# A DMA-bound multiply and GELU: a wider small piece, its x load split in two, and three waits changed

## The chip, the core and the metric

The kernel runs on one core of a Trainium2 chip. The metric is the device time of one execution in microseconds (us). Three runs of the kernel before gave 119.72, 119.79 and 119.87 us; the median is 119.79 us.

## The reference

Two float32 arrays of 1024 x 4096 are multiplied element by element, and the tanh form of GELU is applied to the product.

```
z = x * y
return 0.5 * z * (1 + np.tanh(np.sqrt(2 / np.pi) * (z + 0.044715 * z ** 3)))
```

Each array has 16.78 MB. x and y are read once and the result is written once, so 50.33 MB cross between the chip's DRAM and the core's on-chip memory.

## The kernel before

The kernel treats each array as a flat stretch of 4,194,304 numbers and cuts it into three **pieces**, given in columns of a 128-row tile: piece 0 is columns 0 to 1280, piece 1 is 1280 to 17664, piece 2 is 17664 to 32768 (`PIECES`). A piece is one unbroken stretch of DRAM, and each of the 128 rows (partitions) holds one unbroken part of it. A row of piece 0 is 5 KB long, a row of piece 1 is 64 KB, a row of piece 2 is 59 KB. The trace's records of the DMA traffic have one packet for each row, of that size.

All of x stays on chip, in the tile `xs` of 32768 columns. The products and the GELU are written back into `xs`, and the stores read it. y has a smaller buffer, `ys`, of 20440 columns, so its parts must share room. In the text below x0, x1, x2 are the x loads of pieces 0, 1, 2. y0, y1, y2 are the y loads in their order in `Y_LOADS`, which is another order: y0 belongs to piece 1, y1 to piece 2 and y2 to the small piece 0. The stores o0, o1, o2 follow that same order (`STORES`): piece 1, piece 2, piece 0.

The third number in `Y_LOADS` is the column of `ys` where a part starts. y0 lies at 4056 to 20440. y1 lies at 0 to 15104 and so overlaps y0, and y2 lies at 15104 to 16384. `Y_FREE` says how many products must be done before a y load may be issued: none for y0, three for y1, four for y2.

Two queues issue DMAs. Each DMA is spread over the same 16 DMA engines, and each engine works through the packets of one queue in order.

- ScalarE's queue issues x1 only. `_hoist` moves this issue ahead of the barrier with which the program opens.
- SyncE's queue (SP) issues everything else. x0 is hoisted in the same manner. After the barrier SP waits until x0 has landed, issues y0 and x2, waits for three products, issues y1, waits for the fourth, issues y2, waits for y1's landing (line 114) and for the GELUs of piece 1, issues o0, then o1 and o2 as their GELUs finish. At the end it waits for the stores.

VectorE forms the products (line 98) in the steps of `STEPS`: four steps of 4096 columns for piece 1, seven of 2048 and one of 768 for piece 2, one of 1280 for piece 0. Before a piece's first step it waits for its x and y. ScalarE follows each product with the GELU (line 106). `sem_mul` counts products and `sem_act` counts GELUs; each DMA adds 16 to its semaphore when all of it has landed.

Of the kernel before, what the change touches and what calls it, by code (L numbers as in the profile page):

```python
# [1 line left out]

# [4 lines left out]


F32 = mybir.dt.float32
GELU = mybir.ActivationFunctionType.Gelu_apprx_tanh  # L10

PIECES = [(0, 1280), (1280, 17664), (17664, 32768)]

Y_LOADS = [(1280, 17664, 4056), (17664, 32768, 0), (0, 1280, 15104)]

Y_FREE = [0, 3, 4]

STEPS = [[4096] * 4, [2048] * 7 + [768], [1280]]  # L20
STORES = [(1280, 17664), (17664, 32768), (0, 1280)]
Y_BUF = 20440


def _hoist(nc, issued):

    here = nc.cur_bb.bb.instructions
    first = nc.main_func.blocks[0].instructions
    for ins in issued:
        del here[next(k for k, i in enumerate(here) if i is ins or i.name == ins.name)]  # L30
    engine = issued[0].engine
    at = next(
        k
        for k, i in enumerate(first)
        if i.engine == engine and type(i).__name__ == "InstDrain"
    )
    first[at:at] = issued


@with_exitstack  # L40
def kernel(
    ctx: ExitStack,
    tc: tile.TileContext,
    x: bass.AP,
    y: bass.AP,
    out: bass.AP,
):
    nc = tc.nc
    P = nc.NUM_PARTITIONS

    def columns(t, a, b):

        flat = t.flatten_outer_dims().rearrange("r c -> (r c)")
        pa, pb = next(q for q in PIECES if q[0] <= a and b <= q[1])
        return flat[P * pa : P * pb].rearrange("(p c) -> p c", p=P)[:, a - pa : b - pa]


    tc.close()
    tc.compile()  # L59

    xs = nc.alloc_sbuf_tensor("xs", [P, PIECES[-1][1]], F32).ap()
    ys = nc.alloc_sbuf_tensor("ys", [P, Y_BUF], F32).ap()
    sem_x = [nc.alloc_semaphore(f"sem_x{i}") for i in range(len(PIECES))]
    sem_y = [nc.alloc_semaphore(f"sem_y{i}") for i in range(len(Y_LOADS))]
    sem_mul = nc.alloc_semaphore("sem_mul")
    sem_act = nc.alloc_semaphore("sem_act")
    sem_o = [nc.alloc_semaphore(f"sem_o{i}") for i in range(len(STORES))]

    def load_x(i, engine=nc.sync):
        a, b = PIECES[i]  # L70
        return engine.dma_start(out=xs[:, a:b], in_=columns(x, a, b)).then_inc(sem_x[i], 16)

    def load_y(i):
        a, b, r = Y_LOADS[i]
        return nc.sync.dma_start(
            out=ys[:, r : r + b - a], in_=columns(y, a, b)
        ).then_inc(sem_y[i], 16)

    _hoist(nc, [load_x(0).ins])
    _hoist(nc, [load_x(1, nc.scalar).ins])  # L80
    nc.sync.wait_ge(sem_x[0], 16)
    load_y(0)
    load_x(2)
    for i in range(1, len(Y_LOADS)):
        if Y_FREE[i]:
            nc.sync.wait_ge(sem_mul, Y_FREE[i])
        load_y(i)

    n = 0
    done = {}  # L90
    for i, (a, b, r) in enumerate(Y_LOADS):
        for j, (xa, xb) in enumerate(PIECES):
            if xa <= a < xb:
                nc.vector.wait_ge(sem_x[j], 16)
        nc.vector.wait_ge(sem_y[i], 16)  # L95
        c = a
        for w in STEPS[i]:
            nc.vector.tensor_mul(  # L98
                out=xs[:, c : c + w],
                in0=xs[:, c : c + w],  # L100
                in1=ys[:, r + c - a : r + c - a + w],
            ).then_inc(sem_mul, 1)
            n += 1
            done[c + w] = n
            nc.scalar.wait_ge(sem_mul, n)
            nc.scalar.activation(  # L106
                out=xs[:, c : c + w], in_=xs[:, c : c + w], func=GELU
            ).then_inc(sem_act, 1)
            c += w

    for i, (a, b) in enumerate(STORES):
        if i == 0:
            nc.sync.wait_ge(sem_y[-2], 16)
        nc.sync.wait_ge(sem_act, done[b])
        nc.sync.dma_start(out=columns(out, a, b), in_=xs[:, a:b]).then_inc(sem_o[i], 16)
    for i in range(len(STORES) - 1):
        nc.sync.wait_ge(sem_o[i], 16)
    nums = sorted(s.num for s in [*sem_x, *sem_y, *sem_o[:-1], sem_mul, sem_act])
    assert nums == list(range(nums[0], nums[-1] + 1))
    nc.sync.sem_clear(range(nums[0], nums[-1] + 1))  # L120
    nc.sync.wait_ge(sem_o[-1], 16).then_inc(sem_o[-1], -16)


# [1 line left out]
_INS = ['x', 'y']  # L125
_OUTS = [((1024, 4096), 'float32')]


# [23 lines left out]
```

## Time and profile before

| quantity | value |
|---|---|
| device time, three runs | 119.72, 119.79, 119.87 us |
| span of the profiled execution (first to last instruction) | 118.5 us |
| its own device time | not recorded apart from the three runs; their median lies 1.27 us above its span of 118.52 us |
| VectorE busy | 35.2 us (30%), 13 products |
| ScalarE busy | 31.0 us (26%), 13 GELUs and a table load |
| DRAM read, written | 33.55 MB, 16.78 MB |

The page counts an engine as busy only while it computes. A line such as "xs<-in_x_dram" names what a DMA writes and what it reads. "us to landing" is the time from the issue of a DMA until its semaphore is full, so it includes the time in which the DMA stood behind others in its queue. The trace also holds a record of every DMA packet with start, duration and size, and the time at which each of the 16 engines reported its part of a DMA; where a text speaks of "packet records" or "landings", it means these.

### The profile page before, as it was taken

Reading aid. Unit: us, or ns where it says so; the run is one execution under the profiler, and the core shown is the slowest. Engines: PE = TensorE matmul, PEld = TensorE weight load, DVE = VectorE, ACT = ScalarE, POOL = GpSimd, SP = SyncE. Lnnn points to the kernel's source line nnn. Section 1 sums busy time; section 2 is a strip of 40 time slices with the busy share of each in tenths; the row PEclk is TensorE's granted clock in tenths of the full one; section 3 lists DMA queues with packets and bytes.
Section 4 is the critical chain, followed back from the end, with each engine's and each line's share of the span. In section 5 each row is a group of like instructions: output and inputs, shape, how many; then the busy total and the mean of one; then the engine's idle time right before and its main releaser. Section 6 shows DMA issues by size and latency. Waiting matters only on the chain.

```text
span 118.5 us, 82 instructions
## 1 busy us (share of the span) xinstructions
DVE 35.2 (30%) x13; ACT 31.0 (26%) x14; POOL 0.2 (0%) x4
## 2 busy tenths in 40 slices
DVE  0000000000000069999920000059999940000000
ACT  4000000000000000977975000006998990000000
POOL 0000000000000000000000000000000000000000
DMA  9888899889988897797797797798899887977975
GB/s 492 382 382 382 354 575 487 354 354 398 664 354 354 354 652 326 326 652 326 326 632 347 326 632 347 326 575 354 354 531 531 354 354 326 652 326 326 652 326 221
DMA packets 1296, 50.33 MB, mean 425 GB/s; under 512 B 144, under 2 KB 144, under 8 KB 528
## 3 DMA queue, kind: packets, MB, share of 16 engines
q1 hardware_dynamic: 1152, 41.94, 82.2%
q10 hardware_dynamic: 144, 8.39, 16.5%
HBM read 33.55 MB, written 16.78 MB: 425 GB/s over the span
## 4 chain that ended last, share of the span: by engine, by line
DMA 55%; DVE 24%; ACT 3%; issue 1%; DVEq 0%
DMA ys<-in_y_dram 43%; DVE xs L98 24%; DMA xs<-in_x_dram 11%; ACT xs L106 3%; DVEq L95 0%
## 5 line engine op out<-in xcount | busy, mean ns | idle before, releaser
L98 DVE TENSOR_TENSOR xs<-xs,ys 128x2048 f32<-128x2048 f32 (+3 forms) x13 | 35.2, 2777 | 60.9 <-DMA ys<-in_y_dram 60.9
L106 ACT ACTIVATE xs<-xs 128x2048 f32<-128x2048 f32 (+3 forms) x13 | 29.7, 2301 | 65.1 <-DVE xs L98 65.1
L106 ACT ACT_TABLE_LOAD x1 | 1.3, 1283 | 1.6 <-PEq L59 1.6
L136 POOL MEMSET const-bfloat16-1.0<- 128x1 bf16 x1 | 0.1, 103 | 0.0
L136 POOL MEMSET const-uint8-127<- 128x1 uint8 x1 | 0.1, 102 | 0.0
L136 POOL MEMSET const-float32-0.0<- 128x1 f32 x1 | 0.1, 100 | 0.2 <-issue 0.2
L136 POOL MEMSET const-float32-1.0<- 128x1 f32 x1 | 0.1, 99 | 0.0
## 6 DMA issues: line engine op xcount, KB each, us to landing
xs<-in_x_dram SPq DMA_DIRECT2D x1, 7552.0 KB, 46.5
ys<-in_y_dram SPq DMA_DIRECT2D x1, 7552.0 KB, 22.5
out_dram<-xs SPq DMA_DIRECT2D x1, 7552.0 KB, 20.4
xs<-in_x_dram SPq DMA_DIRECT2D x1, 640.0 KB, 13.6
ys<-in_y_dram SPq DMA_DIRECT2D x1, 640.0 KB, 19.7
out_dram<-xs SPq DMA_DIRECT2D x1, 640.0 KB, 20.8
xs<-in_x_dram ACTq DMA_DIRECT2D x1, 30.4
ys<-in_y_dram SPq DMA_DIRECT2D x1, 29.0
```

Of the source, the lines that this page charges most:

```text
L98: nc.vector.tensor_mul(out=xs[:, c : c + w], in0=xs[:, c : c + w], in1=ys[:, r + c - a : r + c - a + w],).then_inc(sem_mul, 1)
L106: nc.scalar.activation(out=xs[:, c : c + w], in_=xs[:, c : c + w], func=GELU).then_inc(sem_act, 1)
L136: nc = _bacc.Bacc("TRN2", target_bir_lowering=False, num_devices=1)
```

## The change

The small piece grows from 1280 to 4096 columns (rows of 16 KB), and piece 2 shrinks from 15104 to 12288 (rows of 48 KB). Piece 1 keeps its 16384 columns. The hoisted first load of x now brings only the first 1280 columns of each row of piece 0 (the 5 KB **head**); a second DMA brings the other 2816 columns (the 11 KB **tail**). VectorE waits for 32 on that semaphore, which is both. SP no longer waits for x0 before it issues: after the barrier it issues the tail, y0 and x2 one after another. y1 waits for two products in place of three and y2 for three in place of four; the first two products are now 4116 columns wide, so that together they free columns 4056 to 12288, just what y1 overlaps. Before o0, SP now waits for the fifth product in place of y1's landing. There are still 13 products and 13 GELUs.

```
-PIECES = [(0, 1280), (1280, 17664), (17664, 32768)]
+PIECES = [(0, 4096), (4096, 20480), (20480, 32768)]

-Y_LOADS = [(1280, 17664, 4056), (17664, 32768, 0), (0, 1280, 15104)]
+Y_LOADS = [(4096, 20480, 4056), (20480, 32768, 0), (0, 4096, 12288)]

-Y_FREE = [0, 3, 4]
+Y_FREE = [0, 2, 3]

-STEPS = [[4096] * 4, [2048] * 7 + [768], [1280]]
-STORES = [(1280, 17664), (17664, 32768), (0, 1280)]
+STEPS = [[4116, 4116, 4096, 4056], [2048] * 6, [2048, 1280, 768]]
+STORES = [(4096, 20480), (20480, 32768), (0, 4096)]
 Y_BUF = 20440
+
+HEAD = 1280
...
-    def load_x(i, engine=nc.sync):
-        a, b = PIECES[i]
+    def load_x(i, engine=nc.sync, part=None):
+        a, b = part or PIECES[i]
...
-    _hoist(nc, [load_x(0).ins])
+    _hoist(nc, [load_x(0, part=(0, HEAD)).ins])
     _hoist(nc, [load_x(1, nc.scalar).ins])
-    nc.sync.wait_ge(sem_x[0], 16)
+    load_x(0, part=(HEAD, PIECES[0][1]))
     load_y(0)
     load_x(2)
...
-                nc.vector.wait_ge(sem_x[j], 16)
+                nc.vector.wait_ge(sem_x[j], 32 if j == 0 else 16)
...
         if i == 0:
-            nc.sync.wait_ge(sem_y[-2], 16)
+            nc.sync.wait_ge(sem_mul, len(STEPS[0]) + 1)
```

## The prediction, made before the changed kernel ran

> **What bounds the kernel now.** I read the page first, for who is busy, then the chain of waits, then the DMA issues with their landings, then SP's own waits.
>
> The page's slices and its bytes:
>
> ```profile
> span 118.5 us, 82 instructions
> ...
> DMA  9888899889988897797797797798899887977975
> ...
> q1 hardware_dynamic: 1152, 41.94, 82.2%
> q10 hardware_dynamic: 144, 8.39, 16.5%
> HBM read 33.55 MB, written 16.78 MB: 425 GB/s over the span
> ```
>
> The two queues together fill 98.7% of the time of 16 DMA engines. The digits under 9 come from the slices being near one packet in length; no slice is empty. VectorE at 30% and ScalarE at 26% have room.
>
> The chain that ended last, in order of time (start, length, what):
>
> ```profile
> 0.00 13.55 DMA xs<-in_x_dram
> ...
> 13.57 28.99 DMA ys<-in_y_dram
> ...
> 42.66 13.11 DVE xs L98 x3
> ...
> 55.78 22.47 DMA ys<-in_y_dram
> ...
> 78.35 1.53 DVE xs L98
> ...
> 80.56 13.30 DVE xs L98 x6
> ```
>
> This view names x0's wait, the products and y1 as the path. It follows semaphores, and cannot see that the DMA engines have other work during each of these waits. The reader should set it against the landings, which are issue time plus time to landing: x0 13.55, x1 30.48, y0 42.56, x2 60.41, y1 78.25, y2 79.82, o0 99.19, o1 116.98, o2 118.49 us.
>
> ```profile
> xs<-in_x_dram SPq DMA_DIRECT2D x1, 7552.0 KB, 46.5
> ys<-in_y_dram SPq DMA_DIRECT2D x1, 7552.0 KB, 22.5
> ...
> ys<-in_y_dram SPq DMA_DIRECT2D x1, 640.0 KB, 19.7
> ...
> out_dram<-xs SPq DMA_DIRECT2D x1, 640.0 KB, 20.8
> xs<-in_x_dram ACTq DMA_DIRECT2D x1, 30.4
> ys<-in_y_dram SPq DMA_DIRECT2D x1, 29.0
> ```
>
> From y0's landing to x2's, 17.85 us pass for 7.73 MB: 433 GB/s. From x2's to y1's 17.84 us pass for the same bytes, and from y2's to o0's 19.37 us for 8.39 MB: 433 GB/s again. The rate is the same for reads and writes and across every wait of the chain. So the bound is the DMA engines: 50.33 MB at 433.5 GB/s is 116.1 us of 118.5. The other 2.4 us are: 1.0 to 1.5 us until an engine's first packet, 0.46 to 0.52 us lost in the first packets, 0.37 us from the last packet to its landing, and some 0.1 us of small packets. The loss in the first packets is worked out so: when an engine had finished x0 it had moved 8 rows of 5 KB and 4 rows of 64 KB, 11.2 us of work at this rate; the earliest engine stood at 12.66 us, the last at 13.19, so they began in effect at 1.47 and 1.99 us, while their first packets are at 1.01 and 1.49 us. The first packets of 5 KB took up to 756 ns, later ones 196.
>
> SP's own waits:
>
> ```profile
> SPq L75 <- DVE xs L98: 45.4, 2, 41.4
> ...
> SPq L115 <- DMA ys<-in_y_dram: 14.5, 1, 14.5
> SPq L75 <- DMA xs<-in_x_dram: 12.0, 1, 12.0
> ```
>
> The 12.0 us in the last row are the wait that goes. They look dear and are free: x1 keeps all engines at work from 2.3 to 30.1 us, and its packets run without a gap while y0 is not there.
>
> **The change, part by part.** The sum is made for the profiled execution, 118.52 us of span. Its own time is not given apart from the runs; their median stands 1.27 us above the span, and I add that unchanged.
>
> *The wait on x0 goes.* Tail, y0 and x2 are issued after the barrier, from about 1.6 us, one each 0.4 us, as y0 and x2 were (0.34 and 0.43 us of issue). The engines have nothing idle to give: 0 us. What changes is order: x1 now alternates with the tail alone and lands near 24 us (2.4 us, 8 packets of 2.42, and some 1.9 us of heads and tails between them), and y0 lands when x0, x1 and y0 (18.87 MB in place of 17.43) are in: 1.44 MB at 433 GB/s later, 42.56 + 3.33 = 45.9 us. The first product starts 3.3 us later. That is hidden behind x2, whose landing stays at 60.4 us, because by then 25.17 MB have been read in both kernels.
>
> *Two products free y1's room.* Products follow each other at 4.33 us for 4096 columns (GELU starts 47.12, 51.45, 55.78), so 4.35 for 4116. 46.0 + 8.7 = 54.7 us for y1's issue (55.78 before); y2 follows at 59.1. A queue that has run dry needs some 0.84 us from issue to first packet (o0: 78.27 to 79.11), up to 2 us by y0's first round. x2 keeps the engines until 60.0, so y1 has 3 us to spare. With three products it would be 59.1 us, and most of that cover would be gone; so this edit pays for the one before and gains nothing by itself.
>
> *Loads end where they did.* y1, now 6.29 MB, lands at 60.4 + 14.5 = 74.9; y2, now 2.10 MB, at 79.8 us.
>
> *o0 waits for the fifth product.* It starts at 75.0 and takes 2.3 us: issue at 77.4 us, in place of 78.27. Queued behind this wait on SP are only the stores. Its packets can start at 78.2; y2 keeps the engines until 78.9 (first) to 79.4 (last). So the slack is 0.7 us at the first engine and 1.2 at the last; a fifth product that were later than that would cost its whole delay. Before, the early engines did stand idle for up to 0.21 us here (end of y2's packets 78.90, first store packet 79.11). The last engine did not: y2's end at 79.39 and the store at 79.39. The last engine ends the kernel, so curing the idle of the others is worth 0.
>
> *The later stores.* Six products of 2048 at 2.20 us end at 88.3, their GELUs at 90.3; o1 is needed at 99. The last three steps end near 94; o2 is needed at 113.7. Hidden by 9 and 20 us.
>
> *Packet sizes.* Each engine moves the same bytes, in 80 packets in place of 72, with one semaphore packet (9 ns) more. A 5 KB packet takes 196 ns and follows the last after 193, where the 64 KB packets' rate (2416 ns) would give 189: 4 to 7 ns each. Eight more are +0.03 to +0.06 us; o2's 5 KB packets took 200 ns, and 16 KB ones may save about 0.03. No row shows packets of 11, 16 or 48 KB. Bounds: if all 352 KB per engine in 11 and 16 KB packets ran at the 5 KB rate (26.1 bytes per ns against 27.1), the sum would be +0.49 us less the 0.12 us that the 16 dropped 5 KB packets cost: +0.37. If they ran at the 64 KB rate, it would be -0.11. A fixed few ns per packet fits both rows (59 KB took 2229 ns, also the 64 KB rate), so I take +0.02.
>
> A rule against the split: the Trainium skill, "DMA: Bandwidth & Descriptors", section "Bandwidth", wants at least 1 MiB in a DMA and finds 341 GB/s for 1 MB; its anatomy section has about 2.0 us fixed for a DMA issued from GpSimd. If the added DMA paid that, the time would be 121.8 us. The row here speaks otherwise: y2, 0.66 MB behind a filled queue, landed 1.57 us after y1, 417 GB/s. The same page, under "Latency and other measured facts", warns of row pitches at large powers of two, 207 GB/s at 512 KiB; rows 64 KB apart ran at 433 GB/s here, and a pitch of 16 KB no row shows. By that rule the small piece's 6.29 MB would take 30.4 us in place of 14.5, an estimate of 135.7 us in all.
>
> *The opening.* The head's packets are as before, but 16 KB apart in DRAM and not 5. Issues that arrive amid traffic cost little: packets in flight when y0 and x2 were issued took 2425 to 2431 ns against 2418, and 2238 on average when y1 was, against 2229. Now three issues fall between 1.6 and 2.9 us, among the heads. I take 0; bounds are the loss of the first packets once more, +0.5 us, and that loss gone, -0.5.
>
> **Sum:** 118.52 + 0.02 + 1.27 = 119.81 us.
>
> **Rivals.**
>
> *Faster, 119.5 us.* If the early engines' idle does count (0.21 us, were the last engine slowed by the others) and the new packets reach the 64 KB rate (-0.11), the sum is 119.79 - 0.32 = 119.47. For it: the idle is in the packet records. Against it: the last engine ran at its full rate throughout.
>
> *Slower, 120.2 us: a second poor start.* The descriptors of tail, y0 and x2 reach the engines while these still work on short heads. The first heads took up to 756 ns; if the same loss returned in full, it would be +0.5 us, 120.3; at four fifths, 120.2. It decides from 0.24 us, half of the loss. For it: 5 KB packets have little in flight to hide behind. Against it: the 10 ns seen on longer packets.
>
> *Slower through the packet sizes or a late o0:* +0.37 us, 120.16, by the upper bound above; o0 would have to be over 1.2 us late to add to it.
>
> *The change does what it says but nothing bounds there:* this is my forecast.
>
> **How the numbers follow.** About 0.2% (0.24 us) is what a measurement of this kernel can tell from no change. My forecast, a DMA floor that does not move, has 0.42; its own range is 119.57 to 120.03. Faster has 0.25, with the opening's gain in it. Slower has 0.33: 0.23 for the opening, 0.10 for the packet sizes and the store. The range goes from 119.35, a little past the faster rival and short of the opening's full gain, to 120.35, past both slower ones.
>
> **What would show it.** Right: y0 lands near 45.9, x2 near 60.4, y1 near 74.9, y2 near 79.8, o2 near 118.5 us; y1 issued near 54.7 and o0 near 77.4; the queues' shares again near 98.7% together. Wrong in the opening: the gap between y0's landing and 45.9 already holds the whole difference, and the intervals after it are as computed. Wrong in the sizes: y1 to y2 takes other than 4.84 us, or o1 to o2. Wrong on the cover: x2 to y1 takes over 14.5 us, or y2 to o0 over 19.4.

## The result, and the profile after

The changed kernel takes 120.40 us (median of six runs, 120.38 to 120.90) against 119.81 us (119.72 to 119.87) for the kernel before: a ratio of 1.0055, 95% interval 1.0045 to 1.0065. It is slower by 0.55%, or 0.6 us, and just outside the range of 119.35 to 120.35 us. The profiled execution after took 120.47 us with a span of 119.13 us, against 118.52. What lies around the span is 1.3 us, as before, so the loss is inside.

The page after, its span, its slices of DMA work, its queues and its bytes:

```profile
span 119.1 us, 83 instructions
...
DMA  9999899998889989997996996998899889699696
...
q1 hardware_dynamic: 1296, 41.94, 82.1%
q10 hardware_dynamic: 144, 8.39, 16.4%
HBM read 33.55 MB, written 16.78 MB: 422 GB/s over the span
```

The queues still fill 98.5% of the engines' time, and the bytes are the same. The 144 packets more are one DMA of 128 rows with its 16 semaphore packets. The page alone doesn't show where 0.6 us went: packets that take longer count as busy too.

The chain of waits after (start, length, what):

```profile
1.95 44.55 DMA ys<-in_y_dram
...
46.59 8.81 DVE xs L100 x2
...
55.43 20.13 DMA ys<-in_y_dram
...
75.65 4.86 DVE xs L100 x3
```

The DMA issues after (size of the DMA, us from issue to landing):

```profile
xs<-in_x_dram SPq DMA_DIRECT2D x1, 6144.0 KB, 58.5
ys<-in_y_dram SPq DMA_DIRECT2D x1, 6144.0 KB, 20.1
...
xs<-in_x_dram SPq DMA_DIRECT2D x1, 1408.0 KB, 25.6
xs<-in_x_dram SPq DMA_DIRECT2D x1, 640.0 KB, 14.0
xs<-in_x_dram ACTq DMA_DIRECT2D x1, 25.3
ys<-in_y_dram SPq DMA_DIRECT2D x1, 44.6
```

The first chain line is y0: issued at 1.95, landed at 46.50 us, where 45.9 was forecast. Every later landing is late by the same amount and no more: x2 61.03 (forecast 60.4), y1 75.56 (74.9), y2 80.46 (79.8), o0 99.80 (99.2), o2 119.10 (118.5). After y0 the rest of the span takes 119.13 - 46.50 = 72.63 us; by the forecast it was 118.54 - 45.89 = 72.65. So the whole loss is before y0's landing. The 640 KB line narrows it further: the head lands at 14.01 us, where x0, as many bytes in packets of the same size, landed at 13.55. Some 0.46 of the 0.6 us is gone by then.

The packet records give the form of it. The 128 packets of 5 KB took 234 ns on average before and 279 after. In the first rush some are slow in both kernels, but after the change they are slow again at 7.8 us (mean of 16: 255 ns) and at 10.4 us (276 ns), where before all took 196. (The records name no engine; "a group" below is sixteen packets of one DMA in order of their start, one for each engine if all go alike.) Slow packets are not all of it. Those of the small head, of x1 and of y0 sum to 0.40 us more per engine than x0, x1 and y0 before. The rest is mostly time without a packet: between 1 and 3 us, the 16 engines' time less the packets' durations leaves 0.33 us per engine, against 0.19 before. Two things in the change meet there: the head's rows lie 16 KB apart in DRAM, and three more DMAs have been issued by then.

### The profile page after: what moved, and what is told of

Same layout as the page of the kernel before. It is cut to its first block, busy times and chain, and to the rows that moved or that the text cites. A ratio compares the mean times of both kernels' runs of the same rounds, so it can differ in the third digit from the quotient of the medians.

```text
span 119.1 us, 83 instructions
## 1 busy us (share of the span) xinstructions
DVE 35.2 (30%) x13; ACT 31.0 (26%) x14; POOL 0.2 (0%) x4
## 4 chain that ended last, share of the span: by engine, by line
DMA 54%; DVE 19%; ACT 3%; issue 2%; SPq 0%; DVEq 0%
DMA ys<-in_y_dram 54%; DVE xs L100 19%; ACT xs L108 3%; SPq L73 0%; DVEq L97 0%
## 5 line engine op out<-in xcount | busy, mean ns | idle before, releaser
L100 DVE TENSOR_TENSOR xs<-xs,ys 128x2048 f32<-128x2048 f32 (+5 forms) x13 | 35.2, 2778 | 58.2 <-DMA ys<-in_y_dram 58.2
L108 ACT ACTIVATE xs<-xs 128x2048 f32<-128x2048 f32 (+5 forms) x13 | 29.7, 2301 | 62.4 <-DVE xs L100 62.4
## 6 DMA issues: line engine op xcount, KB each, us to landing
xs<-in_x_dram SPq DMA_DIRECT2D x1, 1408.0 KB, 25.6
```

Source lines behind the costliest of these rows:

```text
L100: nc.vector.tensor_mul(out=xs[:, c : c + w], in0=xs[:, c : c + w], in1=ys[:, r + c - a : r + c - a + w],).then_inc(sem_mul, 1)
L108: nc.scalar.activation(out=xs[:, c : c + w], in_=xs[:, c : c + w], func=GELU).then_inc(sem_act, 1)
```

## Experiments

Each ratio below is to the kernel before as measured beside that run (medians of 119.76 to 119.82 us). Where an edit reads other addresses of x, the kernel computes on other elements than the reference does. Theory P: the distance of the rows in DRAM. Theory I: the early issues. The first four runs take each of them out of the changed kernel, and put each into the kernel before.

**e1_wait: the changed kernel, and no issue among the heads**

```
     _hoist(nc, [load_x(1, nc.scalar).ins])
+    nc.sync.wait_ge(sem_x[0], 16)
     load_x(0, part=(HEAD, PIECES[0][1]))
```

> The changed kernel, with one wait more: after the barrier SP waits until the 5 KB head has landed, and only then issues the tail, y0 and x2. Theory I (the three issues among the heads cost the 0.6 us): back to 119.85 us, and y0 lands near 45.95 us. Theory P (the heads' rows lie 16 KB apart in DRAM and are read more slowly, whenever the others are issued): stays at 120.4 us, y0 near 46.5 us.

Measured: 120.49 us, ratio 1.0056 (1.0041 to 1.0071). The head lands at 13.88, the tail, issued only then, at 27.05, y0 at 46.41 us. Two lines of its chain, x0's head and y0:

```profile
0.00 13.88 DMA xs<-in_x_dram
...
14.28 32.14 DMA ys<-in_y_dram
```

With nothing issued among the heads the loss is still there, so theory I doesn't explain it.

**e4_nowait: the kernel before, without its wait on x0**

```
-    nc.sync.wait_ge(sem_x[0], 16)
     load_y(0)
     load_x(2)
```

> The kernel before, with SP's wait on x0 taken out, so that y0 and x2 are issued right after the barrier; nothing else is changed. Theory I: slower by 0.3 to 0.5 us, 120.1 to 120.3. Theory P: 119.81 us, and x0's packets at 234 ns.

Measured: 119.82 us, ratio 1.0001 (0.9991 to 1.0010); x0 lands at 13.41 and y0 at 42.43 us (42.56 before):

```profile
1.57 40.86 DMA ys<-in_y_dram
```

The wait of 12 us that the change takes away is worth nothing either way. Theory I is refuted from both sides.

**e3_pitch: the kernel before, x0's rows 16 KB apart**

```
         flat = t.flatten_outer_dims().rearrange("r c -> (r c)")
+        if t is x and b == 1280:
+            return flat[0 : P * 4096].rearrange("(p c) -> p c", p=P)[:, 0:b]
```

> The kernel before, but x0's 5 KB rows are read 16 KB apart; other elements of x than the reference's. The wait on x0 stays, so nothing is issued among these packets. Theory P: 120.3 us (+0.5), 5 KB packets of x0 near 279 ns. Theory I: 119.81 us, 234 ns.

Measured: 120.62 us, ratio 1.0065 (1.0050 to 1.0080). Only the DRAM addresses of 0.66 MB have changed, and this loss is somewhat more than that of the whole change. x0 lands at 14.21 us (13.55 before), y0 at 43.33 (42.56):

```profile
xs<-in_x_dram SPq DMA_DIRECT2D x1, 640.0 KB, 14.2
...
xs<-in_x_dram ACTq DMA_DIRECT2D x1, 31.1
ys<-in_y_dram SPq DMA_DIRECT2D x1, 29.1
```

x0's packets average 257 ns, where 279 was expected, and x1 suffers too: its second to fourth groups average 2469 to 2482 ns where before they averaged 2418 to 2439. Between 1 and 3 us the engines are without a packet for 0.45 us each (0.19 before).

**e2_dense: the changed kernel, the head from an unbroken stretch**

```
         flat = t.flatten_outer_dims().rearrange("r c -> (r c)")
+        if t is x and b == HEAD:
+            return flat[0 : P * b].rearrange("(p c) -> p c", p=P)
```

> The changed kernel, but the head is read from one unbroken stretch of DRAM, rows 5 KB apart, as x0 was in the kernel before; these are other elements of x, so the head's columns are not those of the reference. Issues as in the changed kernel. Theory P: 119.85 us, head packets back to a mean of some 234 ns, y0 near 45.95 us. Theory I: stays at 120.4 us with head packets near 279 ns.

Measured: 120.56 us, ratio 1.0062 (1.0045 to 1.0079). Theory P as it stood is wrong here: the head is cured (landing 13.57, packets 227 ns on average) and the time is not. The DMA issues of e2_dense, first the tail (11 KB rows, still 16 KB apart), then the head:

```profile
xs<-in_x_dram SPq DMA_DIRECT2D x1, 1408.0 KB, 25.7
xs<-in_x_dram SPq DMA_DIRECT2D x1, 640.0 KB, 13.6
```

Head and tail show 13.6 and 25.7 here, 14.0 and 25.6 in the changed kernel: with a better start the tail ends no earlier. In the packet records the tail's 11 KB packets take 422 ns each in the changed kernel, all 128 of them; in e2_dense those from the third group on average 488 to 585 ns, and x1's last two groups 2432 and 2482. So the loss has moved: here, as in the changed kernel, the first DMA with rows 16 KB apart pays, and in the changed kernel the next one, the tail, doesn't. The theory was mended to P2: 16 KB rows run into each other while the engines go in step, and this pushes the engines apart in time, after which they run freely. The next run tests whether the rows are the cause, not how they come to cost.

**e5_bothdense: head and tail each from an unbroken stretch**

```
+        if t is x and b == HEAD:
+            return flat[0 : P * b].rearrange("(p c) -> p c", p=P)
+        if t is x and a == HEAD:
+            return flat[P * a : P * b].rearrange("(p c) -> p c", p=P)
```

> The changed kernel, but head and tail are each read from an unbroken stretch of DRAM (rows 5 KB and 11 KB apart); the small piece of x then has other elements than the reference's. Everything else of the change stays: no wait, 16 KB rows in y2 and o2, o0 behind the fifth product. Theory P2 (the first DMA whose rows lie 16 KB apart is slow, until the engines have come out of step; with a dense head it is the tail that pays): 119.85 us, y0 near 45.95, tail packets 422 ns. Theory T (the tail is slow because a second short DMA stands beside x1, whatever its rows): 120.5 us, y0 near 46.6, tail packets over 480 ns.

Measured: 119.91 us, ratio 1.0008 (0.9999 to 1.0017). Its DMA issues:

```profile
xs<-in_x_dram SPq DMA_DIRECT2D x1, 1408.0 KB, 25.1
xs<-in_x_dram SPq DMA_DIRECT2D x1, 640.0 KB, 13.6
...
ys<-in_y_dram SPq DMA_DIRECT2D x1, 44.1
```

y0 lands at 46.00 us and all tail packets take 422 ns. Everything of the change is in this kernel but the distance of x's small rows, and about 0.5 of the 0.6 us is back. A second short DMA beside x1 costs little or nothing by itself. y2's and o2's rows still start 16 KB apart in it, and cost nothing there (614 and 611 ns a packet, as in the changed kernel); but those rows are 16 KB long, so they lie end to end and leave no gaps, which head and tail did.

P2's reason stays unshown, and two records do not fit it. The head's landings are spread over 0.65 us in e2_dense, where the tail then pays, and over 0.50 us in the changed kernel, where it doesn't: being apart did not protect it. And in e1_wait a group of x1's packets that starts at 13.1 us averages 2520 ns (2418 in e5_bothdense), though the head's last packet has ended at 11.1 us and the tail's first starts at 18.1. So some 0.1 us is paid while no row with gaps is in flight.

**e12_split: the same, as a kernel that computes the reference.** The small piece is laid out as two unbroken stretches for x, y and out, so y2 and o2 become two DMAs each.

```
-        pa, pb = next(q for q in PIECES if q[0] <= a and b <= q[1])
+        pa, pb = next(q for q in [(0, HEAD), (HEAD, 4096), *PIECES[1:]] if q[0] <= a and b <= q[1])
...
+        for c, d in [(0, HEAD), (HEAD, 4096)] if a == 0 else [(a, b)]:
```

> The changed kernel with its small piece laid out as two unbroken stretches, 1280 and 2816 columns, for x, y and out alike: y2 and o2 become two DMAs each, one of 5 KB and one of 11 KB rows. It computes the reference. All else of the change stays. If the 16 KB distance is the cause: 119.85 us, y0 near 46.0. If the two added DMAs cost more than their 8 packets an engine each (some 0.03 us): over 120.0 us.

Measured: 119.95 us, ratio 1.0019 (1.0009 to 1.0028); y0 lands at 45.87 us, as forecast for the change itself:

```profile
1.95 43.91 DMA ys<-in_y_dram
```

Some 0.2 us stay, part of which the two added DMAs may cost; that wasn't taken apart. It beats the changed kernel and not the one before.

**Which distances.** Five runs repeat e3_pitch with other distances; the edit is that of e3_pitch with 2048, 3840, 4352, 8192 or 16384 columns in place of 4096.

> The kernel before with x0's 5 KB rows read 17 KB apart (other elements of x than the reference's). Power of two: 119.81 us, x0 lands near 13.55. Rows apart, whatever the distance: 120.6 us, x0 near 14.2, as with 16 KB.

> The kernel before with x0's 5 KB rows read 32 KB apart (other elements of x than the reference's). Power of two: at least as slow as 16 KB apart, 120.6 us or more, x0 lands at 14.2 or later. Rows apart, whatever the distance: 120.6 us.

> The kernel before with x0's 5 KB rows read 8 KB apart (other elements of x than the reference's). Theory S (16 KB is a bad distance by itself, any other costs at most the 0.3 us that 17 and 32 KB cost): 119.8 to 120.15 us. Theory M (small powers of two are bad, 32 KB was already beyond): 120.5 us or more.

> The kernel before with x0's 5 KB rows read 15 KB apart (other elements of x than the reference's). Theory S: 120.1 us, as with 17 KB, x0 landing by 13.9. If all distances near 16 KB are bad for the span they cover: 120.5 us; but 17 KB speaks against that.

> The kernel before with x0's 5 KB rows read 64 KB apart, the distance of x1's own rows (other elements of x than the reference's). Theory S: 120.1 us, as with 32 KB. If the loss comes from x0 and x1 meeting in step: 120.6 us, with x1's packets of 64 KB slow beyond the first of each engine.

| x0's rows apart | time, us | ratio to before (95%) | x0 lands, us |
|---|---|---|---|
| 5 KB (before) | 119.81 | 1 | 13.55 |
| 8 KB | 120.58 | 1.0074 (1.0057 to 1.0091) | 13.96 |
| 15 KB | 119.93 | 1.0014 (1.0005 to 1.0023) | 13.67 |
| 16 KB | 120.62 | 1.0065 (1.0050 to 1.0080) | 14.21 |
| 17 KB | 120.14 | 1.0026 (1.0017 to 1.0036) | 13.85 |
| 32 KB | 120.14 | 1.0028 (1.0016 to 1.0041) | 13.70 |
| 64 KB | 120.26 | 1.0044 (1.0029 to 1.0059) | 13.85 |

8 and 16 KB are the worst, though the intervals of 16 and 64 KB overlap. It is not the stretch of DRAM that the rows span: 15 and 17 KB span nearly the same as 16 and cost far less. Neither theory held whole: not all powers of two are equally bad, and every other distance costs something as well. The packet records show two kinds of loss. At 15, 17, 32 and 64 KB only packets of the first 6 us are slow, most of them in the first 3; from 6.5 us on x0's packets take 196 to 197 ns and x1's 2419 to 2421 on average. At 8 and 16 KB x0's packets stay slow to their end, at 11 us, and x1's until about 16 us. The time without a packet between 1 and 3 us sorts in the same way: 0.40 and 0.45 us per engine at 8 and 16 KB, 0.20 to 0.28 at the other four.

**e6_rows17: the changed kernel with rows of 17 KB**

```
-PIECES = [(0, 4096), (4096, 20480), (20480, 32768)]
+PIECES = [(0, 4352), (4352, 20736), (20736, 32768)]
```

`Y_LOADS`, `STORES` and the later `STEPS` follow.

> The changed kernel with a small piece of 4352 columns in place of 4096 (rows of 17 KB; piece 2 has 12032 columns, rows of 47 KB). It computes the reference. Theory P2 with the power of two as its cause: 119.85 us, head packets near 234 ns, y0 near 46.2 us (0.13 MB more before it). If it is only that the head's rows are apart from each other: 120.4 us, y0 near 46.8.

Measured: 120.05 us, ratio 1.0021 (1.0012 to 1.0030), y0 at 46.24 us:

```profile
1.95 44.29 DMA ys<-in_y_dram
```

One more KB in a row takes back 0.35 of the 0.6 us, and some 0.2 us stay. The profiled execution was the fastest of the ten (119.93 us), and y0 lands in it as forecast, so no trace shows where those 0.2 us lie.

**e13_alone16 and e14_alone: x0 without x1 beside it.** What stayed open was whether the 16 KB rows collide with each other or with x1's packets. Both kernels hold x1 back until x0 has landed, and e13_alone16 has the edit of e3_pitch besides.

```
-    _hoist(nc, [load_x(1, nc.scalar).ins])
     nc.sync.wait_ge(sem_x[0], 16)
+    load_x(1)
```

> The kernel before with x0's 5 KB rows read 16 KB apart (other elements of x than the reference's) and with x1 taken out of the opening: SP issues x1 after x0 has landed, so x0 runs alone. The time is several us longer for that. To be read: the duration of x0's packets and x0's landing. If the 16 KB rows are slow among themselves: the packets stay slow past the first of each engine, mean over 270 ns, and x0 lands at least 0.4 us later than in e14_alone. If they are slow only because they meet x1's packets: about the same as e14_alone past the first packets.

> The kernel before with x1 taken out of the opening in the same way and x0's rows 5 KB apart as ever. It computes the reference. Both theories: x0's packets near 196 ns past the first of each engine, x0 lands near 3.1 us. It is what e13_alone16 is read against.

The start of the chain of waits, of e14_alone and then of e13_alone16:

```profile
0.00 3.50 DMA xs<-in_x_dram
```

```profile
0.00 4.03 DMA xs<-in_x_dram
```

x0 alone lands 0.53 us later with its rows 16 KB apart, and the single runs differ by 0.42 us (122.14 and 122.56). With x1 alongside the landing moved by 0.66 us and the kernel by 0.8. So a good part of the loss comes without any packet of x1; how much can't be read closely from single runs. Past the first group the mean is 220 ns against 199, short of the 270 that was expected: the second to fifth groups are slow (215 to 281 ns), and the last three take 196. The landings are spread over 0.90 us, where e14_alone has 0.35. That would fit collisions which separate the engines and then stop, as P2 says, but it doesn't show them. And x0 alone is over by 3.7 us, within the stretch in which every distance of the table makes packets slow. So the pair leaves open whether what sets 8 and 16 KB apart, the slow packets after that, needs x1.

## Why the prediction was wrong

**The step that failed is the one on the opening.** It said: "the head's packets are as before, but 16 KB apart in DRAM and not 5", and "I take 0", with bounds of 0.5 us both ways. The term measured +0.6 us (y0 at 46.50 against 45.89). It saw the distance and priced it at nothing; the bound was a little short, and the range, cut at 120.35, missed 120.40. That this distance is the cause is shown: e5_bothdense takes some 0.5 us back by it alone, e12_split 0.4 with the rows of y2 and o2 split as well, and e3_pitch adds 0.8 us to the kernel before. How the rows come to cost it stays open. The sign that the prediction gave for an error in the opening came as written: y0 is late by the whole difference, and the intervals after it are as computed.

**The slower rival had the sign and nearly the size but not the mechanism, so its sign was luck.** "A second poor start" forecast 120.2 to 120.3 us and blamed the descriptors of three DMAs arriving among short heads. e1_wait and e4_nowait show these to cost nothing that can be measured. The row set against it was the better guide: packets in flight during y0's and x2's issues were slower by some 10 ns.

**The reasons given against the distance were rows from another situation.** The prediction set a warning of the Trainium skill ("DMA: Bandwidth & Descriptors", section "Latency and other measured facts": row pitches at large powers of two) against x1's 64 KB rows at 433 GB/s, and passed on. But x1's rows are as long as their distance, so they lie end to end; e11_pitch64 shows 5 KB rows at those same 64 KB costing 0.5 us. The page's rate isn't what happens here either: the tail's rows, 11 KB of every 16, took 422 ns a packet in the changed kernel, 427 GB/s for 16 engines. What does happen is a loss of 0.6 to 0.8 us, paid once, at the first DMA of the opening whose short rows lie 8 or 16 KB apart. The same section's remedy, a pitch padded by a few KiB, agrees with e6_rows17 in direction: one KB more, and 120.05 in place of 120.40 us.

**The rest of the sum held.**

- The wait on x0: forecast 0; e4_nowait 1.0001.
- y1's issue: forecast 54.7, measured 55.43, 0.7 later, of which 0.6 is y0's; x2's landing hides it, as said. x2 to y1 takes 14.53 us (14.5 forecast).
- o0's issue: 77.4 forecast, 77.97 measured. y2 to o0 takes 19.35 us (19.37 before), so curing the early engines' idle was worth no more than the 0 it was given.
- Packet sizes: 11 KB packets take 422 ns, 16 KB ones 611 to 614, 48 KB ones 1815, which is some 6 to 9 ns above the rate of the 64 KB packets (2418 ns) for the small two and 1 to 2 for the large. The bound of +0.37 us was far off; the +0.02 fits the 72.63 us after y0 (72.65 forecast) and the 0.1 us that e5_bothdense leaves. y1 to y2 takes 4.90 us (4.84 forecast).
- Two readings on the way were off, and the sum didn't rest on them: x1 was to land near 24 us after the change and landed at 25.44, and before it x1's last packet ended at 27.7 us, not 30.1.

The change had nothing to gain: what it removed was hidden, as predicted. It became slower through an address distance, which no wait shows and which the busy share of 98.5% hides.

## What to carry to other kernels

When a change moves where rows start in DRAM, cost that by itself, above all for the DMAs of the opening; the steady rate of a long transfer whose rows lie end to end doesn't answer it, whatever their distance. If the first landing is late and all later intervals are as before, look at packets and addresses of the opening, not at waits. And undo such a cause in all its places: with the head alone cured, the tail paid the same amount.

## What the runs showed of the hardware that was not expected

- x0's 5 KB rows cost least when unbroken (5 KB apart). At 15 KB apart the kernel takes 0.14% more, at 17 KB 0.26%, 32 KB 0.28%, 64 KB 0.44%, 16 KB 0.65%, 8 KB 0.74%.
- The loss at 16 KB ends by itself: the tail's rows, with the same distance and gaps, took 422 ns a packet throughout when the head had paid, and 488 to 585 from the third group on when it had not. That the engines drift apart, and that this ends it, is argued and not shown; the spread of the landings in e2_dense speaks against it, and the engines' phase wasn't set by hand.
- Part of the loss is not slow packets but engines without any: 0.33 to 0.46 us per engine between 1 and 3 us in the kernels with short rows 8 or 16 KB apart in the first DMA, 0.11 to 0.28 in the others with x1 alongside.
- Why 8 and 16 KB are bad and 32 and 64 KB less so stays open, as does why packets of the first 3 us are slower on average at every distance tried than at 5 KB.
